# Second attention of a two-block network: two heads per step on the halves of TensorE's array, sums and factors of the head norms in fewer products

## The chip, the cores and the metric

One Trainium2 chip, one of its cores. The metric is device time in microseconds (us) of one execution, the median of three runs. TensorE (PE) does matrix products out of SBUF into PSUM banks (512 fp32 per partition each), VectorE (DVE), ScalarE (ACT) and GpSimd (POOL) work element by element, SyncE (SP) issues the transfers. Each engine executes its own instruction list strictly in the order that the scheduler wrote when the kernel was built, and waits on semaphores for the others.

## The reference, cut to what matters

Two blocks of a network over 256 tokens of 1024 features. The first (two layers of differential attention, a gated recurrence, a Fourier mixer and a feed-forward part) isn't touched. The second is a gated convolution and then this attention, `D` = 1024, 16 head slots of 64 features, three groups of dilation 1, 4 and 16:

```python
proj = h @ w_in
qkv = proj[..., :QKV_COLS].reshape(B, S, N_GROUPS, 3, HEADS_PER_GROUP, HEAD_DIM)
for g, (window, dilation) in enumerate(DILATED_GROUPS):
    q = rms_norm_2(qkv[:, :, g, 0], q_gain[g])     # norm over the 64 features of a head
    k = rms_norm_2(qkv[:, :, g, 1], k_gain[g])
    o, l = dilated_group_attention(q, k, qkv[:, :, g, 2], bias_g, window, dilation)
alpha = jax.nn.softmax(jnp.stack(lses, axis=0), axis=0)
o = jnp.sum(alpha[..., None] * jnp.stack(outs, axis=0), axis=0)
y = o.reshape(B, S, ATTN_WIDTH) * jax.nn.silu(z)
return y @ w_out
```

The merge by `alpha` equals one softmax over the keys of all three groups, and so the kernel computes it.

## The kernel before, in words

The whole kernel is one stream of large products (`gemm`, L160, and `gemm_nat`, L171): every fp32 weight is split into a high part `wH` (ACT, L138) and a low part `wL` (DVE, L140), every activation too, and a product is the sum of three fp32r products, each one record of 256 columns in this part of the kernel. The weights come by SP's queue as 512 KB halves `raw`.

`attn2` is the last part. After the gates `szz` it goes through four steps `hq` of four heads each (two pairs `i`, the heads `v` = 0, 1 of a pair in partitions 0 to 63 and 64 to 127). For each of the three groups `g` of a step:

- Queries and keys `qk` by `gemm` into a `pg` bank, ACT squares them (`sqq`), and the sums of the squares over each head's 64 features are products with the 0/1 matrix `hsel` (L1081): four products of 32 output columns, one for each pair of heads of queries and keys, two behind the queries and two behind the keys, into partitions 0, 32, 64 and 96 of a bank of `ph`.
- The values `vv` by `gemm_nat`.
- From the sums DVE makes `ms` (L1091), POOL and ACT the reciprocal root `mr` with one Newton step (L1092 to L1101), ACT and DVE split it into two parts `r` (L175, L176), and eight products with `bsel` (L1108; two parts for each of four) spread each factor over the 64 partitions of its head, into both banks of `ph`. DVE multiplies: `qhat` (L1110), `khat` (L1113).

Then the attention of the step, eight units (pair `i`, half `qt` of the query tokens, head `v`). `scores` (L1117 on) makes four fp32 products of 128 columns (`qt` = 0, "early" units below) or one of 256 and two of 128 (`qt` = 1, "late") from the 64 partitions of head `v` into a `ps` bank (there are two), DVE adds the bias tile `bt` and takes the maximum (L1133), ACT takes the exponential (L1137), DVE scales by the reciprocal of the sum (L1138, L1139): `lt`. `values` (L1142 on) transposes `lt` on PE (L1149), ACT copies it to `aT` (L1151), and four fp32 products (L1153) give 64 output partitions, `64 v` on, of the bank `pa`. Each unit's `values` is emitted one unit later than its `scores`. An fp32 product is two records ("passes") in the trace, an fp32r product or a transpose one.

The output projection `merge` (L1033 on; L160 with `yo`) of steps 0 to 2 adds into `x` (L1038, one add for six products), that of step 3 comes last (L1051, L1054).

The order on each engine is the scheduler's, from the emission order and its own estimate of when things are ready: it puts large products of the next step between the small ones of the attention. Step 3's attention has no next step; only the merges of steps 0 to 2 (24 tiles of six products) stand there to fill.

Of the kernel before, what the change touches and what calls it, by code (L numbers as in the profile page):

```python
# [9 lines left out]
F32 = mybir.dt.float32  # L10
# [36 lines left out]
for _n, _w in (("hsel", 32), ("bsel", 512)):  # L47
# [11 lines left out]
class Builder:  # L59
# [27 lines left out]
    def phase(self, *groups):  # L87
        """tags of ring() and how many tiles each has; memory goes to one group after the other"""
# [34 lines left out]
    # ---------------------------------------------------------------- weights  # L123
# [18 lines left out]
    def wload(self, src, nk=8, w=256, hold=((None, None),) * 2):  # L142
        """weights of nk * 128 rows and w columns; hold: instructions of ACT and DVE that go before each half"""
# [7 lines left out]
    def gemm(self, W, c0, acts, T, t0=0, pt=None, tag=None):  # L151
        """transposed output [128 columns, T tokens from t0]"""
# [11 lines left out]
    def gemm_nat(self, W, acts, t0, pt, p0):  # L164
        """natural output [128 tokens from t0, 256 columns]"""
# [12 lines left out]
    # ---------------------------------------------------------------- norms  # L178
# [10 lines left out]
    def sums(self, pn, c0, acc):  # L189
        """sums over the features, one per token, into columns c0.. of pn; acc = [128, 2 tiles, 128 tokens]"""  # L190
# [3 lines left out]
    def inv(self, name, src):  # L194
        """1 / sqrt(src / 1024 + eps), [128, 2]"""
# [7 lines left out]
    def spread(self, r):  # L203
        """one value per token, [128, 2], to [128, 256] on all partitions, in PSUM"""
# [13 lines left out]
    # ---------------------------------------------------------------- setup  # L218
# [26 lines left out]
    def late_setup(self):  # L245
# [12 lines left out]
        # lambda of both layers  # L258
# [13 lines left out]
        # lower bound of the forget gate in layer 1: softmax over the two layers  # L272
# [35 lines left out]
    def ada_bank(self, li, b):  # L308
        """columns 1024b.. of the modulation of layer li, for c and c_ctx"""
# [13 lines left out]
    def ada_out(self, li, pa, tiles, n):  # L323
        """n feature tiles from tiles[g] on in partitions 32g and 32g + 1"""
# [12 lines left out]
    def ada_scale(self, li, which, A, k0, k1):  # L337
        """norm weight times (1 + scale), [128, 2 sequences, 8], for feature tiles k0..k1"""
# [8 lines left out]
    def norm(self, pb, v, k, tag):  # L347
        """feature tiles k and k + 1 of the 256 tokens of sequence v, normalised"""
# [6 lines left out]
    def modulate(self, n, v, k, A, Bm, h):  # L355
        """scale and shift of what norm() gives, into high and low parts"""
# [12 lines left out]
    # ---------------------------------------------------------------- recurrent mixer  # L369
    def hgrn_seq(self, j, s, fg, kk, q, vs, S0):  # L370
        """one sequence of 256 tokens of head pair j. fg, kk: forget gates and keys, forward and backward;
        q: queries, None where only the state is wanted. Scores of tokens that part at level h of the binary
        tree over the tokens are products of a query that carries the decay from the middle of its block of 2h
        and a key that carries the decay up to there. Returns the scores' products with the values.
        K: keys with the decay to the end (plane 0) or the start (plane 1) of their block of h; Q: queries with
        the decay from the end (plane 0) or the start (plane 1); tot: products of the gates over blocks of h
        (forward, backward, forward)."""
        nc = self.nc

        def view(t, h, off, plane, bc=False):  # L380
            """[P, 2 planes, blocks of 2h, h]: half a block of each plane"""
# [4 lines left out]
        def sel(t, h, t0=0, nt=256):  # L386
            """nt tokens from t0, first halves of the blocks from plane 0 and second halves from plane 1"""
# [3 lines left out]
        def level(h, t, tots, eng):  # L391
            """blocks of 2h from blocks of h"""
# [67 lines left out]
        if s == 1:  # L460
            # state at the end of the context
# [30 lines left out]
    def hgrn(self, li, j, fg, kk, q, sg, vn, T):  # L492
# [8 lines left out]
        # head norm and gate  # L501
# [10 lines left out]
    # ---------------------------------------------------------------- first block layer  # L512
    def layer(self, li, states):
# [74 lines left out]
        def rec(j, tag=None):  # L588
            w = first[0][0] if li == j == 0 else W(8 + 2 * j)  # both forget gates of head pair j
# [12 lines left out]
            w = first[1][0] if li == j == 0 else W(6 + j)  # query and gate of head pair j  # L602
# [760 lines left out]
```

## Time and profile before

| | |
|---|---|
| median of 3 runs (lowest to highest) | 1795.1 us (1791.59 to 1797.15) |
| span of the profiled execution, first to last instruction | 1791.7 us; no time of its own is listed beside it, the lowest of the three runs is the same to 0.1 us |
| PE busy | 1731.3 us, 97% of the span |
| DVE, ACT, POOL busy | 57%, 47%, 18% |
| mean granted TensorE clock | 0.984 of 2.4 GHz |
| the chain that ended last | PE 88%, DMA 3%, DVE 3% |
| `attn2`: first product on step 0 to the last add | about 1440 to 1788 us |

A record's duration is its latency, with pipeline; what a product costs a stream of products is the distance between starts.

### The profile page before, as it was taken

What the parts mean: (1) busy time and instruction counts of PE and PEld (TensorE: products, weight loads), DVE (VectorE), ACT (ScalarE), POOL (GpSimd) and SP (SyncE); (2) the same over time, 40 slices, a digit from 0 to 9 for tenths busy, and PEclk for the clock granted to TensorE, in tenths of its full rate; (3) what the DMA queues carried; (4) which work ended last, traced back from release to release, by engine and by line L of the source; (5) the groups of instructions that cost most, each with busy time, mean ns of one, the idle gap of its engine ahead of it and who ended that gap; (6) DMA issues with size and microseconds to landing.
All of it is one profiled execution on the core that took longest, in us unless ns stands there. A gap on an engine that the chain in (4) does not pass through costs nothing.

```text
span 1791.7 us, 29942 instructions
## 1 busy us (share of the span) xinstructions
PE 1731.3 (97%) x11966; PEld 1478.6 (83%) x11966; DVE 1021.4 (57%) x1849; ACT 849.3 (47%) x1481; POOL 316.2 (18%) x412
## 2 busy tenths in 40 slices
PE   6999999888999999989999999999999999999998
PEld 3876666676878888878877899999999999898987
DVE  4457564444543454365775766777666745554646
ACT  4457454334432343254654655664444655554543
POOL 1322210121100011234310210122111202111120
PEclk9999999988999999989999899999999999999999
DMA  9433433675233222453246456465555554344441
GB/s 346 166 106 121 135 113 127 180 108 164 91 97 109 94 95 67 131 180 106 92 137 226 140 159 211 149 198 187 182 187 182 180 174 157 123 133 134 147 130 54
DMA packets 88804, 260.66 MB, mean 145 GB/s; under 512 B 8887, under 2 KB 20535, under 8 KB 88664
## 3 DMA queue, kind: packets, MB, share of 16 engines
q1 hardware_dynamic: 88664, 258.74, 45.6%
q8 instruction: 94, 1.54, 0.4%
q14 instruction: 46, 0.38, 0.1%
HBM read 252.42 MB, written 6.29 MB: 144 GB/s over the span
## 4 chain that ended last, share of the span: by engine, by line
PE 88%; DMA 3%; DVE 3%; ACT 2%; SPq 2%; issue 1%; POOL 0%; POOLq 0%; ACTq 0%; DVEq 0%
PE pg L160 35%; PE ps L160 15%; PE pu L160 8%; PE ph L160 8%; PE pg L171 7%; PE pa L319 3%; DMA araw<-in_w_ada_dram 2%; PE pa L1153 2%; PE ph L442 1%; PE ps L698 1%; PE pu L1149 1%; SPq L316 1%; PE ph L1081 1%; PE ph L1108 1%; PE pu L736 1%
## 5 line engine op out<-in xcount | busy, mean ns | idle before, releaser
L140 DVE TENSOR_TENSOR wL<-raw,wH 128x1024 fp32r<-128x1024 f32 (+2 forms) x388 | 447.2, 1180 | 286.8 <-ACT wH L138 277.8
L138 ACT CAST wH<-raw 128x1024 fp32r<-128x1024 f32 (+2 forms) x388 | 372.4, 994 | 415.9 <-PE pg L160 178.4
L160 PE MATMUL pg<-hx,wH 128*128 128x256 f32 x1152 | 215.7, 283 | 0.0
L160 PE MATMUL pg<-hm,wH 128*128 128x512 f32 (+1 forms) x736 | 209.4, 366 | 1.8 <-DVE hm L366 0.7
L160 PEld LDWEIGHTS pg<-hx,wH 128*128 128x128 f32 x1152 | 178.9, 188 | 2.5 <-issue 1.6
L160 PE MATMUL pg<-hx,wL 128*128 128x256 f32 x576 | 164.1, 285 | 0.0
L160 PEld LDWEIGHTS pg<-hm,wH 128*128 128x128 f32 x736 | 129.9, 192 | 41.4 <-issue 13.7
L160 PE MATMUL pg<-hm,wL 128*128 128x512 f32 (+1 forms) x368 | 132.4, 360 | 0.0
L160 PE MATMUL pg<-h,wH 128*128 128x256 f32 (+1 forms) x464 | 116.8, 340 | 10.4 <-ACT wH L138 8.7
L843 POOL TENSOR_TENSOR tt<-tt 128x512 f32<-128x512 f32 (+1 forms) x44 | 44.6, 1013 | 438.0 <-DVE tt L840 432.7
L160 PE MATMUL ps<-h,wH 128*128 128x256 f32 (+1 forms) x464 | 114.5, 335 | 0.0
L160 PEld LDWEIGHTS pg<-hx,wL 128*128 128x128 f32 x576 | 108.5, 188 | 5.7 <-issue 5.4
L160 PEld LDWEIGHTS pg<-h,wH 128*128 128x128 f32 x464 | 81.1, 193 | 21.8 <-ACT wH L138 9.2
L160 PEld LDWEIGHTS ps<-h,wH 128*128 128x128 f32 x464 | 80.3, 191 | 9.5
L160 PE MATMUL pg<-hid,wH 128*128 128x256 f32 (+1 forms) x360 | 81.1, 316 | 1.1 <-ACT wH L138 1.1
L160 PEld LDWEIGHTS pg<-hm,wL 128*128 128x128 f32 x368 | 70.5, 192 | 13.9 <-issue 5.0
L319 PE MATMUL pa<-araw,csil 128*32 128x256 f32 x640 | 64.7, 406 | 15.1 <-DMA araw<-in_w_ada_dram 14.5
L160 PE MATMUL pg<-h,wL 128*128 128x256 f32 (+1 forms) x232 | 78.5, 338 | 0.0
L160 PE MATMUL ps<-hid,wH 128*128 128x256 f32 (+1 forms) x344 | 77.7, 317 | 0.0
L160 PE MATMUL ps<-h,wL 128*128 128x256 f32 (+1 forms) x232 | 77.5, 334 | 0.0
L171 PE MATMUL pg<-wH,hx 128*128 128x256 f32 x384 | 76.1, 285 | 0.0
L160 PE MATMUL pu<-h,wH 128*128 128x256 f32 (+1 forms) x272 | 68.7, 339 | 4.8 <-ACT wH L138 4.8
(417 smaller groups left out, 3874.5 us busy)
## 6 DMA issues: line engine op xcount, KB each, us to landing
raw<-in_w_up_dram SPq DMA_DIRECT2D x88, 512.0 KB, 4.7
araw<-in_w_ada_dram SPq DMA_DIRECT2D x80, 512.0 KB, 5.2
raw<-in_attn_w_in_dram SPq DMA_DIRECT2D x80, 512.0 KB, 4.6
raw<-in_conv_w_in_dram SPq DMA_DIRECT2D x64, 512.0 KB, 4.6
raw<-in_w_in_dram SPq DMA_DIRECT2D x48, 512.0 KB, 4.8
raw<-in_w_down_dram SPq DMA_DIRECT2D x32, 384.0 KB, 3.5
raw<-in_w_down_dram SPq DMA_DIRECT2D x32, 320.0 KB, 2.9
raw<-in_conv_w_out_dram SPq DMA_DIRECT2D x16, 512.0 KB, 4.5
```

The source lines that it names most:

```text
L138: nc.scalar.copy(H[:, a:b], raw)
L140: nc.vector.tensor_tensor(L[:, a:b], raw, H[:, a:b].bitcast(F32), OP.subtract)
L160: nc.tensor.matmul(pt, a[:, k, c0:c0 + P], c[:, t0:t0 + T], start=n == 0, stop=n == tot - 1)
L171: nc.tensor.matmul(pt[:, p0:p0 + 256], c[:, t0:t0 + P], a[:, k, :], start=n == 0, stop=n == tot - 1)
L316: nc.sync.dma_start(raw, d["w_ada"][li, k * P:(k + 1) * P, b * 1024:(b + 1) * 1024] .rearrange("p (g c) -> p g c", g=4))
L319: nc.tensor.matmul(pa[32 * g:32 * g + 32, 0:256], self.csil[:, k, :], raw[:, g], start=k == 0, stop=k == KD - 1)
L442: nc.tensor.matmul(pt[:, v, c:c + P], l, m, start=True, stop=True)
L698: nc.tensor.matmul(pts[i][:, :n], qa[h][rr, qt * P:(qt + 1) * P], kT[h][rr, k0 * P:k0 * P + n], start=True, stop=True)
L736: nc.tensor.matmul(po[:, 0:P], aT[:, b * P:(b + 1) * P], va[kb // 2][:, kb % 2, hh * P:(hh + 1) * P], start=b == 0, stop=b == nk - 1)
L843: nc.gpsimd.tensor_tensor(tt[1], tt[0], tt[1], OP.mult)
L1081: nc.tensor.matmul(pc[32 * n:32 * n + 32, 0, 0:256], hsel, sq[:, a], start=True, stop=True)
L1153: nc.tensor.matmul(pavs[i][64 * v:64 * v + 64, qt * P:(qt + 1) * P], vv[g][:, kt, (i * 2 + v) * 64:(i * 2 + v) * 64 + 64], aT[:, k * P:(k ...
```

## The change

1. Two heads per step of the attention: `scores` and `values` now take a unit (`i`, `qt`) and do both heads `v`, their products emitted alternately. `scores` takes both `ps` banks. `values` puts the transposes of both heads into the two banks of `ph`, one `aT` tile holds both (two tiles of 4 KB in place of three of 2 KB), and the products into `pa` alternate between output partitions 0 to 63 and 64 to 127.
2. The four products of the sums are emitted together, behind the products of the values, into a `pu` bank (`sqq` gets a third buffer).
3. `hsel` puts every sum into two rows (columns 0, 1 and 16, 17 of 32). `rl` = `rh` times `low` plus `r`, with `low` 0 for the first copy and -1 for the second, holds the rounded factor in one row and the remainder in the other, so that one product with a `bsel` that has ones in both rows does what two did: four spread products for a group in place of eight. They go into `pu`, one bank for the queries and then one for the keys, where both lay in `ph` before.
4. The constant tile `cc` gets one column more (`low`).

The core of the diff (docstrings and comments were dropped elsewhere):

```diff
-        self.phase(dict(szz=4, qk=3, sqq=2, qhat=6, khat=6, vv=6, lt=4, aT=3, yo=8))
+        self.phase(dict(szz=4, qk=3, sqq=3, qhat=6, khat=6, vv=6, lt=4, aT=2, yo=8))
...
-                    sq = self.ring("sqq", [P, 2, 256])
-                    nc.scalar.activation(sq, raw[i], AF.Square)
-                    for a in range(2):
-                        n = 2 * i + a
-                        nc.tensor.matmul(pc[32 * n:32 * n + 32, 0, 0:256], hsel, sq[:, a], start=True, stop=True)
+                    sq.append(self.ring("sqq", [P, 2, 256]))
+                    nc.scalar.activation(sq[i], raw[i], AF.Square)
                 w = W(g * 12 + 8 + hq)
                 pt = self.pg()
                 t = self.ring("vv", [P, 2, 256])
                 for a in range(2):
                     self.gemm_nat(w, acts, a * P, pt, a * 256)
+                pc = self.psum("pu")
+                for n in range(4):
+                    nc.tensor.matmul(pc[32 * n:32 * n + 32, 0:256], hsel, sq[n // 2][:, n % 2], start=True, stop=True)
+                for a in range(2):
                     nc.scalar.activation(t[:, a], pt[:, a * 256:(a + 1) * 256], AF.Copy, scale=rs[:, a:a + 1])
...
-                pc = self.psum2().rearrange("p n (i t) -> p n i t", i=2)
-                rh = [self.loc(f"r{i}", [P, 256], F32R, bufs=2) for i in range(2)]
-                self.split(rh[0], rh[1], r)
-                for n in range(2):
+                rh = self.loc("r0", [P, 256], F32R, bufs=2)
+                nc.scalar.copy(rh, r)
+                rl = self.loc("r1", [P, 256], F32R, bufs=2)
+                nc.vector.scalar_tensor_tensor(rl, rh.bitcast(F32), low, r, op0=OP.mult, op1=OP.add)
+                for n, (name, gain, to) in enumerate((("qhat", g8[:, g:g + 1], qh), ("khat", self.vec("kg", g), kh))):
+                    pc = self.psum("pu")
                     for i in range(2):
-                        for c in range(2):
-                            nc.tensor.matmul(pc[:, n, i], bsel[:, 2 * n + i], rh[c], start=c == 0, stop=c == 1)
...
-            def scores(i, v, qt, b):
-                ps = self.psum("ps")
+            def scores(i, qt, bt):
+                ps = [self.psum("ps") for _ in range(2)]
                 qs = slice(qt * P, qt * P + P)
...
+                for g, o, ks in parts:
+                    for v in range(2):
+                        nc.tensor.matmul(ps[v][:, o:o + ks.stop - ks.start], qh[g][rr[v], i, qs], kh[g][rr[v], i, ks],
+                                         start=True, stop=True)
...
-                pt = self.psum2()[:, 0] if hq == 3 and len(done) % 2 else self.psum("pu")
-                for k in range(4):
-                    nc.tensor.transpose(pt[:, k * P:(k + 1) * P], lt[:, k * P:(k + 1) * P], self.ident)
-                aT = self.ring("aT", [P, 512])
-                nc.scalar.copy(aT, pt)
+                pt = self.psum2()
+                aT = self.ring("aT", [P, 2, 512])
+                for v in range(2):
+                    for k in range(4):
+                        nc.tensor.transpose(pt[:, v, k * P:(k + 1) * P], lts[v][:, k * P:(k + 1) * P], self.ident)
+                    nc.scalar.copy(aT[:, v], pt[:, v])
                 for k, (g, kt) in enumerate(blocks):
-                    nc.tensor.matmul(pavs[i][64 * v:64 * v + 64, qt * P:(qt + 1) * P],
-                                     vv[g][:, kt, (i * 2 + v) * 64:(i * 2 + v) * 64 + 64],
-                                     aT[:, k * P:(k + 1) * P], start=k == 0, stop=k == 3)
+                    for v in range(2):
+                        nc.tensor.matmul(pavs[i][64 * v:64 * v + 64, qt * P:(qt + 1) * P],
+                                         vv[g][:, kt, (i * 2 + v) * 64:(i * 2 + v) * 64 + 64],
+                                         aT[:, v, k * P:(k + 1) * P], start=k == 0, stop=k == 3)
```

The order of the instructions changes on PE and on DVE within `attn2`, and nowhere ahead of it. The first place is the attention of step 2 on PE, first pair, with the large products between them left out. Before (the number behind `ps` tells the banks' tiles, one for each head):

```order
L1123 MATMUL ps_16571<-khat_16083,qhat_16081 128x256
L1129 MATMUL ps_16571<-khat_16305,qhat_16303 128x128
L1129 MATMUL ps_16571<-khat_16527,qhat_16525 128x128
L1123 MATMUL ps_16594<-khat_16083,qhat_16081 128x256
L1129 MATMUL ps_16594<-khat_16305,qhat_16303 128x128
L1129 MATMUL ps_16594<-khat_16527,qhat_16525 128x128
```

Now, at the same late unit, and then at the late unit of the second pair:

```order
L1129 MATMUL ps_16516<-khat_16046,qhat_16041 128x256
L1129 MATMUL ps_16516<-khat_16265,qhat_16260 128x128
L1129 MATMUL ps_16516<-khat_16484,qhat_16479 128x128
...
L1129 MATMUL ps_16517<-khat_16046,qhat_16041 128x256
L1129 MATMUL ps_16517<-khat_16265,qhat_16260 128x128
L1129 MATMUL ps_16517<-khat_16484,qhat_16479 128x128
...
L1129 MATMUL ps_16616<-khat_16046,qhat_16041 128x256
L1129 MATMUL ps_16616<-khat_16265,qhat_16260 128x128
L1129 MATMUL ps_16616<-khat_16484,qhat_16479 128x128
L1112 MATMUL pu_16895<-r1_16893,bsel_13835 128x256 x2
...
L1129 MATMUL ps_16617<-khat_16046,qhat_16041 128x256
```

The code emits the products of the two heads alternately, but the list holds all of one head and then all of the other, with one large product between them at the first unit shown, two spread products and 20 large ones at the second. Over the four steps the stretches of score products between other work number 28 before and 35 now.

The second place is a unit's values on PE, the same step, now:

```order
L1155 MATMUL ph_16541<-ca_71,lt_16508 128x128 x4
L1159 MATMUL pa_16540<-aT_16542,vv_15966 64x128
...
L1159 MATMUL pa_16540<-aT_16542,vv_15966 64x128
L1159 MATMUL pa_16540<-aT_16542,vv_16185 64x128 x2
L1159 MATMUL pa_16540<-aT_16542,vv_16404 64x128 x2
L1159 MATMUL pa_16540<-aT_16542,vv_15966 64x128 x2
```

The first of the eight products is issued alone, behind the transposes, and the other seven, which alternate, some 30 rows later. So it is in 15 of the 16 units; in the last all eight stand together. Before, each of the 32 units had its four products in one stretch.

The third place is the end of PE's list, behind the last merge tile of step 2. Now:

```order
L1052 MATMUL pg<-yo,wH 128x256 x2
L1052 MATMUL pg<-yo,wL 128x256
L1159 MATMUL pa<-aT,vv 64x128 x7
L1155 MATMUL ph<-ca,lt 128x128 x8
L1159 MATMUL pa<-aT,vv 64x128 x8
L1052 MATMUL ps<-yo,wH 128x256
```

Before, the last values were spread among the products of the merges:

```order
L1153 MATMUL pa<-aT,vv 64x128 x4
L1051 MATMUL ps<-yo,wL 128x256
L1051 MATMUL ps<-yo,wH 128x256
L160 MATMUL pg<-yo,wH 128x256 x2
L160 MATMUL pg<-yo,wL 128x256
L160 MATMUL pg<-yo,wH 128x256 x2
L160 MATMUL pg<-yo,wL 128x256
L1051 MATMUL ps<-yo,wH 128x256
```

Now all products with the first half of `yo` stand ahead of the last seven products of one unit, and between the last transposes, the last values and the last 24 products nothing else is left.

## Rows read from the trace of the kernel before

**Rows 1.** The page: its head, and PE's busy time with share and records.

```profile
span 1791.7 us, 29942 instructions
PE 1731.3 (97%) x11966; PEld 1478.6 (83%) x11966; DVE 1021.4 (57%) x1849; ACT 849.3 (47%) x1481; POOL 316.2 (18%) x412
```

**Rows 2.** Windows up to step 3's last sums, and behind them: length, busy time (records).

```profile
1453.30:1737.70 284.40, 284.40 (x2267) 257.99 (x2265) 146.24 (x244) 148.75 (x248) 49.91 (x66) 1.00 0.43 139
1737.70:1791.70 54.00, 46.70 (x363) 41.30 (x359) 34.59 (x86) 19.01 (x36) 5.80 (x6) 0.99 0.22 72
```

**Rows 3.** Timeline of PE around two of the sums' products: start, us, records.

```profile
1453.33 0.28 PE L171 MATMUL pg<-wH,hx 128*128 128x256 f32 x1
1453.54 0.62 PE L1081 MATMUL ph<-sqq,cc 128*32 128x256 f32 x4
1454.10 0.38 PE L171 MATMUL pg<-wL,hx 128*128 128x256 f32 x1
1454.32 0.40 PE L171 MATMUL pg<-wH,hx 128*128 128x256 f32 x2
1454.55 0.28 PE L171 MATMUL pg<-wL,hx 128*128 128x256 f32 x1
```

**Rows 4.** Timeline of PE around the values of one head in step 3.

```profile
1777.81 0.39 PE L1051 MATMUL ps<-yo,wH 128*128 128x256 f32 x2
1778.13 1.09 PE L1153 MATMUL pa<-aT,vv 128*64 128x128 f32 x8
1779.15 0.50 PE L160 MATMUL pg<-yo,wH 128*128 128x256 f32 x2
1779.49 0.28 PE L160 MATMUL pg<-yo,wL 128*128 128x256 f32 x1
```

**Rows 5.** Timeline of PE in the recurrence: products alternating between output halves, first and last.

```profile
124.11 0.44 PE L487 MATMUL ph<-Sd,vh 128*64 128x128 f32 x4
...
124.81 0.39 PE L487 MATMUL ph<-So,vh 128*64 128x128 f32 x4
```

**Rows 6.** Timeline of PE in the modulation: four neighbouring tiles of 32 columns.

```profile
163.26 1.06 PE L319 MATMUL pa<-araw,csil 128*32 128x256 f32 x12
```

**Rows 7.** Timeline of PE: late scores of two heads, one behind the other.

```profile
1752.03 0.28 PE L160 MATMUL pg<-yo,wL 128*128 128x256 f32 x1
1752.24 0.70 PE L1123 MATMUL ps<-khat,qhat 64*128 64x256 f32 x2
...
1753.85 0.51 PE L160 MATMUL pg<-yo,wH 128*128 128x256 f32 x2
1754.19 0.28 PE L160 MATMUL pg<-yo,wL 128*128 128x256 f32 x1
```

**Rows 8.** Timeline of PE: late scores of one head alone.

```profile
1529.02 0.36 PE L171 MATMUL pg<-wH,hx 128*128 128x256 f32 x1
1529.31 0.70 PE L1123 MATMUL ps<-khat,qhat 64*128 64x256 f32 x2
...
1530.38 0.38 PE L171 MATMUL pg<-wL,hx 128*128 128x256 f32 x1
1530.61 0.28 PE L171 MATMUL pg<-wH,hx 128*128 128x256 f32 x1
```

**Rows 9.** Waits of PE from 1737.7 us on: in total, times, longest.

```profile
PE ph L1108 <- ACT r L175: 1.4, 1, 1.4
PE pg L160 <- DVE x L1038: 0.8, 2, 0.5
```

**Rows 10.** Timeline of DVE: factors of step 3's last group, from sums to split.

```profile
1738.11 0.42 DVE L1091 SCALAR_TENSOR_TENSOR ms<-ph,Rb 128x256 f32<-128x256 f32 x1 [1.26 <-PE ph L1081]
...
1746.05 0.42 DVE L176 TENSOR_TENSOR r<-mr,r 128x256 fp32r<-128x256 f32 x1 [0.39 <-ACT r L175]
```

**Rows 11.** Groups of DVE from 1737.7 us on: busy us, mean ns, idle time before.

```profile
L140 DVE TENSOR_TENSOR wL<-raw,wH 128x1024 fp32r<-128x1024 f32 x6 | 7.5, 1270 | 0.2 <-ACT wH L138 0.2
L1133 DVE CUSTOM_DVE_ANT_0 lt<-ps,bt 128x512 f32<-128x512 f32 x8 | 5.3, 684 | 0.7 <-PE ps L1129 0.7
...
L1158 DVE TENSOR_TENSOR y<-pa,szz 128x256 f32<-128x256 f32 x2 | 0.8, 424 | 2.3 <-PE pa L1153 2.3
```

More of the change, by code (lines that the diff above doesn't have):

```diff
@@ L46 @@
 _ncc = 0
-for _n, _w in (("hsel", 32), ("bsel", 512)):
+for _n, _w in (("hsel", 32), ("bsel", 512), ("low", 1)):
     _CC[_n] = (_ncc, _ncc + _w)
@@ new lines, in attn2 @@
+                nc.scalar.copy(rh, r)
[3 more added lines that the diff above has]
+                    pc = self.psum("pu")
+                    for i in range(2):
+                        nc.tensor.matmul(pc[:, i * 256:(i + 1) * 256], bsel[:, 2 * n + i], rl, start=True, stop=True)
+                    o = self.ring(name, [P, 2, 256])
+                    nc.vector.scalar_tensor_tensor(o.rearrange("p i t -> p (i t)"), raw[n].rearrange("p i t -> p (i t)"),
+                                                   gain, pc, op0=OP.mult, op1=OP.mult)
+                    to.append(o)
@@ L1119, in scores @@
+            def scores(i, qt, bt):
+                ps = [self.psum("ps") for _ in range(2)]
                 qs = slice(qt * P, qt * P + P)
-                rr = slice(64 * v, 64 * v + 64)
-                lq = [qh[g][rr, i, qs] for g in range(3)]
+                rr = [slice(64 * v, 64 * v + 64) for v in range(2)]
                 if qt:
-                    nc.tensor.matmul(ps[:, 0:256], lq[0], kh[0][rr, i, :], start=True, stop=True)
+                    parts = [(0, 0, slice(0, 256))] + [(g, (g + 1) * P, qs) for g in (1, 2)]
@@ L1124, in scores @@
                 else:
-                    nc.tensor.matmul(ps[:, 0:128], lq[0], kh[0][rr, i, 0:P], start=True, stop=True)
-                    nc.tensor.matmul(ps[:, 384:512], lq[0], kh[0][rr, i, P:256], start=True, stop=True)
-                for g in (1, 2):
-                    o = (g + 1 if qt else g) * P
-                    nc.tensor.matmul(ps[:, o:o + P], lq[g], kh[g][rr, i, qs], start=True, stop=True)
-                lt = self.ring("lt", [P, 512])
-                mx = self.sml("mx", [P, 2], bufs=4)
@@ L1132, in scores @@
-                bb = (b[:, 0:4] if qt else b[:, 1:5]).rearrange("p a c -> p (a c)")
-                nc.vector.tensor_tensor_reduce(out=lt, in0=ps, in1=bb, scale=1.0, scalar=-3.0e38, op0=OP.add,
-                                               op1=OP.max, accum_out=mx[:, 0:1])
-                nc.vector.tensor_scalar(mx[:, 1:2], mx[:, 0:1], -1.0, None, op0=OP.mult)
-                Z = self.sml("Z", [P, 2], bufs=4)
-                nc.scalar.activation(lt, lt, AF.Exp, bias=mx[:, 1:2], accum_out=Z[:, 0:1])
@@ L1138, in scores @@
-                nc.vector.reciprocal(Z[:, 1:2], Z[:, 0:1])
-                nc.vector.tensor_scalar(lt, lt, Z[:, 1:2], None, op0=OP.mult)
-                return lt
-            def values(i, v, qt, lt):
-                if v == 0 and qt == 0:
+                    parts = [(0, 0, slice(0, P)), (0, 384, slice(P, 256))] + [(g, g * P, qs) for g in (1, 2)]
+                for g, o, ks in parts:
+                    for v in range(2):
+                        nc.tensor.matmul(ps[v][:, o:o + ks.stop - ks.start], qh[g][rr[v], i, qs], kh[g][rr[v], i, ks],
+                                         start=True, stop=True)
@@ new lines, in scores @@
+                lts = []
+                for v in range(2):
+                    lt = self.ring("lt", [P, 512])
+                    mx = self.sml("mx", [P, 2], bufs=4)
+                    bb = (bt[v][:, 0:4] if qt else bt[v][:, 1:5]).rearrange("p a c -> p (a c)")
+                    nc.vector.tensor_tensor_reduce(out=lt, in0=ps[v], in1=bb, scale=1.0, scalar=-3.0e38, op0=OP.add,
+                                                   op1=OP.max, accum_out=mx[:, 0:1])
+                    nc.vector.tensor_scalar(mx[:, 1:2], mx[:, 0:1], -1.0, None, op0=OP.mult)
+                    Z = self.sml("Z", [P, 2], bufs=4)
+                    nc.scalar.activation(lt, lt, AF.Exp, bias=mx[:, 1:2], accum_out=Z[:, 0:1])
+                    nc.vector.reciprocal(Z[:, 1:2], Z[:, 0:1])
+                    nc.vector.tensor_scalar(lt, lt, Z[:, 1:2], None, op0=OP.mult)
+                    lts.append(lt)
@@ L1163, in attn2 @@
             sz = szs[hq]
-            pavs, prev, bt, done = {}, None, {}, []
-            for u in [(i, v, qt) for i in range(2) for qt in range(2) for v in range(2)] + [None]:
-                lt = None
+            pavs, prev, bt = {}, None, {}
+            for u in [(i, qt) for i in range(2) for qt in range(2)] + [None]:
+                lts = None
                 if u:
-                    i, v, qt = u
+                    i, qt = u
                     if qt == 0:
-                        bt[v] = bias_tile(hq * 4 + i * 2 + v)
-                    lt = scores(i, v, qt, bt[v])
+                        bt = [bias_tile(hq * 4 + i * 2 + v) for v in range(2)]
+                    lts = scores(i, qt, bt)
                 if prev:
                     values(*prev)
-                prev = (*u, lt) if u else None
+                prev = (*u, lts) if u else None
         for hq in range(4):
@@ L1263, in _constants @@
     cc = np.zeros((P, _ncc), f)
-    cc[0:64, 0] = 1
-    cc[64:128, 1] = 1
-    for n in range(4):
-        for v in range(2):
-            cc[32 * n + v, 32 + n * P + 64 * v:32 + n * P + 64 * v + 64] = 1
+    for v in range(2):
+        for half in range(2):
+            cc[64 * v:64 * v + 64, 16 * half + v] = 1
+            for n in range(4):
+                cc[32 * n + 16 * half + v, 32 + n * P + 64 * v:32 + n * P + 64 * v + 64] = 1
+    cc[:, 544] = np.where(i % 32 < 16, 0, -1)
     bk = _buckets()
```

20 lines of the change are left out of this document (8 added, 12 removed).

## Prediction

> **What bounds the kernel now.** I read the page first, then windows, the timeline of PE and the waits. The page shows PE busy for 97% of the span [rows 1]; a busy share alone doesn't say that PE's work sets the end. The windows do: from the first sums of `attn2` to the last ones of step 3 PE is busy for 284.40 of 284.40 us, while DVE and ACT work half of the time [rows 2]. There a product saved is time saved, as long as what PE needs next is there. Behind these sums the step without a next step remains: 54.00 us, PE busy for 46.70 [rows 2], some of it waits: 1.4 us for the factors and 0.8 us for adds [rows 9]. So I count PE's work for all of `attn2`, and then ask what waits appear in the last step.
>
> The price of an operation on PE is not its duration but the distance between starts, and a stretch of products on a part of the array pays for entering and leaving. Large products follow each other at 0.117 us: two from 1454.32 to 1454.55 [rows 3].
>
> **Sums.** From 1453.33 to 1454.32 stand two large products and one group of two sums' products: 0.99 less 0.23 is 0.75 us for a group [rows 3]. There are 24 groups (12 times two), 18.0 us. Now four products stand together, in 12 groups, one of them cut in two: 13 stretches. Do four neighbours cost more than two? The modulation puts four tiles of 32 columns side by side, and twelve passes took 1.06 us there, one alone being 0.4 [rows 6]; two at a time they would be six rounds of some 0.22, 1.5 us with the pipeline. So four go together, and a stretch costs 0.75 as before. Bounds: 0.75 and twice its inner part, 1.2. I take 0.75, the row being of the same shape: 24 x 0.75 - 13 x 0.75 = **8.2 us saved** (with 1.2: 2.4).
>
> **Spread.** 96 products become 48, full array, at the stream's pace: 48 x 0.117 = **5.6 us saved**. The keys' two must now wait until DVE has emptied the one bank (`qhat`). In steps 0 to 2, 20 to 28 large products stand between in PE's list, 2.3 us or more, and cover that; in the last step it is counted below.
>
> **Values.** From 1777.81 to 1779.49 stand four large products and one head's eight passes: 1.68 - 0.47 = 1.21 us [rows 4]. In the recurrence the products already alternate between output halves: from the first row of four passes to the last are twelve passes in 0.70 us, six slots of 0.117 for two passes each [rows 5]. So two heads take the slots of one, if they alternate. Eight slots are 0.9 us, so entering and leaving cost 0.3. Now PE's list has, for 15 of 16 units, one product alone (two slots and a switch, 0.2 + 0.3 = 0.5) and then seven, whose busier half has eight passes (1.2); the last unit has all in one stretch. Before 32 x 1.21 = 38.7, now 15 x 1.75 + 1.21 = 27.5: **11.2 us saved**. Bounds: were it no overlap, 15 x 2.7 + 2.2 = 42, 4 lost; without the cut, 19.4 saved. The row [rows 5] is the same form, so the upper part of this is unlikely.
>
> The Trainium skill, TensorEngine Tiling (Array Packing), section Theoretical Speedup, gives up to twice the speed for a dimension of 64 or less; under Key Properties it also says that a change of the tiling mode drains the engine. By the first alone the values would save 19.4 us and the total would be some 8 us lower; the trace agrees with the second (the 0.3 us for each stretch, rows 4), and that is why the cut costs most of the difference.
>
> **Scores.** The diff alternates the heads, the list doesn't: it has all of one head, large products, and then the other, except at the first unit of a step. What it costs: two heads in succession took 1752.03 to 1754.19, less three large products, 1.81 us [rows 7], since the second head starts while the first still runs; one head alone 1529.02 to 1530.61, less two, 1.36 [rows 8]. Eight slots being 0.9, a switch is 0.45 here. Before, 28 stretches: 8 with one product for each head (estimate 0.3 + 0.45 = 0.75), 6 with one head (1.36), 8 with two heads in succession (1.81), 6 others (about 1.0): 6.0 + 8.2 + 14.5 + 6.0 = 34.7. Now 35: 7 at 0.75, 16 with one head (1.36), 1 in succession, 5 alternating with three products each (0.65 + 0.45), 6 others at about 0.85: 5.3 + 21.8 + 1.8 + 5.5 + 5.1 = 39.5. That is 4.8 lost. Tiled stretches border on each other in 14 places now against 4, and share a switch of about 0.2: 2.0 back. **2.8 us lost.** Were they alternating in one stretch each, 16 x 1.36 = 21.8, 13 saved: that is a bound, which the list excludes.
>
> Transposes keep their number and their groups of four; the split on DVE, the copies, the exponentials keep shapes and counts. One column more in `cc` is loaded before the convolution, far from use. On SP's queue the last two bias tiles of a step now follow each other, with a weight half less between; the fourth waits for a reduction, and weights behind it with it. PE's work without any wait up to 1737.7 [rows 2] says that weights come with room; were it used up, this belongs to the second rival.
>
> PE's work: -8.2 - 5.6 - 11.2 + 2.8 = **-22.2 us**.
>
> **The last step.** Its factors take from the sums' products until 1746.47 (1746.05 + 0.42; `ms` began at 1738.11), 8.4 us [rows 10]. Until the first spread product PE's list has eight merge tiles and one stretch of scores now, 48 x 0.117 + 0.9 = 6.5, so some 1.5 to 2 us of wait, in place of 1.4 before [rows 9]. From the first spread product to the next unit's scores, which need the second bank, DVE's list has two splits of weights (1.27), two reductions (0.68), `qhat` and `khat` (taken as 0.68, the same 512 columns) and four adds (taken as 0.42, the 256 columns of L1158) [rows 11], 6.9 us in all, where PE's has six merge tiles (4.2), the spread (0.5) and a stretch of scores (0.75): 1.4 us of waits. At the very end PE's list has transposes, copy, last values, and then nothing: 0.9 us for the copy and 1.4 for `y` (0.42 [rows 11]), its cast and its subtraction, which before lay beside merges. Some 5.3 in place of 2.2: **3 us lost**.
>
> **Sum.** 1791.7 - 22.2 + 3 = 1772.5 for the span. The median of the runs lies 3.4 us above the profiled span (1795.1 against 1791.7): 1776. Within 0.3% (5.4 us) a measurement of this kernel can't tell a change from none.
>
> **The rivals.**
> - *As above*, 1768 to 1783: chance 0.67.
> - *Waits in steps 0 to 2.* PE works strictly in order, and each unit's scores now want both `ps` banks, each unit's transposes both banks of `ph`. If PE waits 0.7 us for each of these 12 units (a reduction's length, rows 11), 8 us are given back: 1784. Against it, nothing waited there before [rows 2], and the list leaves large products between most. Chance 0.15 (1783 to 1789).
> - *Less switching than I count*: values that take half, the cut costing nothing, save 8 us more: 1768; with no extra waits in the last step also 1765. Chance 0.08 (1760 to 1768). The 0.3 us of a stretch [rows 4] speak against it. The factor of two of the Trainium skill's TensorEngine Tiling (Array Packing), Theoretical Speedup, would come out as this case.
> - *Slower, by DVE's queue.* In front of the reduction that frees the second bank stand another reduction and a weight's split: 0.68 + 1.27 = 1.95 us. If PE waits for that at each of the 16 units, 31 us go, 12 more than the gain: 1807. It decides from 1.2 us per unit on (19 over 16). In the list that queue stands so in the last step only, four units. Chance 0.04.
> - *No overlap: the change doesn't do what it says.* Values lose 4, sums save 2.4 at most, spread saves 5.6, scores lose 3, the last step 3: 1797. Rows 5 and 6 show overlap in this kernel. Chance 0.01; the rest, 0.05, for small mixtures that end within 0.3%.
>
> **Chances and range.** Slower by over 0.3%: 0.04; within: 0.05; faster: 0.91. The range takes the first case, most of the second and the upper part of the third: 1766 to 1787.
>
> **What would show it.** Right: sums in some 13 stretches of 0.75 us; 48 spread products; a unit's seven products in 1.0 us from first to last start, starts in pairs; scores of a head in 1.3 us, no pairs, except at a step's first unit; PE full up to the last sums, and these about 18 us earlier than 1737.7; more wait behind them. Wrong: waits of PE on DVE's `mx` or `lt` in steps 0 to 2; eight slots that take 1.8 us; sums of four that take 1.2.

## The result, and the profile after

The changed kernel takes 1777.57 us (median of 4 runs, 1775.45 to 1778.72), the kernel before, run beside it, 1793.59 us (4 runs, 1791.59 to 1797.15). The ratio is 0.9908, with a 95% interval of 0.9896 to 0.9921: 16 us less. The profiled execution took 1775.45 us, with a span of 1773.6. The page of the changed kernel, its head and PE's row, which answer to [rows 1]:

```profile
span 1773.6 us, 29835 instructions
PE 1707.7 (96%) x11918; PEld 1462.1 (82%) x11918; DVE 1018.5 (57%) x1849; ACT 846.3 (48%) x1481; POOL 320.8 (18%) x412
```

The windows of the changed kernel up to the last sums of step 3, and behind them, with the columns of [rows 2]:

```profile
1460.80:1721.50 260.70, 260.70 (x2181) 239.74 (x2180) 142.30 (x242) 142.78 (x244) 54.25 (x66) 1.00 0.46 149
1721.50:1773.60 52.10, 43.38 (x356) 37.77 (x348) 34.71 (x86) 19.15 (x37) 5.06 (x6) 0.98 0.20 65
```

PE is still full up to the last sums, at a granted clock of 1.00, its upper level, and these come 16.2 us earlier (1721.5 against 1737.7). Behind them the span is 1.9 us shorter, though PE is idle for longer (8.7 us against 7.3 [rows 2]). All waits of PE in the attention lie there:

```profile
PE pg L160 <- DVE x L1039: 1.3, 3, 0.7
PE ps L1052 <- ACT yo L175: 1.0, 1, 1.0
PE ph L1155 <- ACT aT L1156: 0.7, 1, 0.7
PE pg L160 <- ACT vv L1089: 0.5, 1, 0.5
PE pa L1159 <- ACT aT L1156: 0.3, 1, 0.3
```

They add up to 3.8 us. In the kernel before they are 2.5: the two rows of [rows 9], 2.2, and a third that [rows 9] doesn't show:

```profile
PE pg L160 <- ACT vv L1087: 0.3, 1, 0.3
```

Before the last sums there is none in either kernel. Behind them, PE's list from the sums to the first spread product, and DVE's from the sums to the factors' second part:

```profile
1721.20 0.64 PE L1087 MATMUL pu<-sqq,cc 128*32 128x256 f32 x8
1721.77 0.94 PE L1129 MATMUL ps<-khat,qhat 64*128 64x128 f32 x12
...
1729.84 0.40 PE L1112 MATMUL pu<-r,bsel 128*128 128x256 f32 x2
```

```profile
1721.91 0.42 DVE L1093 SCALAR_TENSOR_TENSOR ms<-pu,Rb 128x256 f32<-128x256 f32 x1 [2.91 <-PE pu L1087]
...
1729.10 0.48 DVE L1108 SCALAR_TENSOR_TENSOR r<-r,cc,mr 128x256 fp32r<-128x256 f32 x1
```

Now the prices, from the timeline of PE (start, us, operation, records). Four sums side by side, in place of the two of [rows 3]:

```profile
1460.63 0.28 PE L171 MATMUL pg<-wH,hx 128*128 128x256 f32 x1
1460.84 0.64 PE L1087 MATMUL pu<-sqq,cc 128*32 128x256 f32 x8
1461.40 0.51 PE L160 MATMUL pg<-hx,wH 128*128 128x256 f32 x2
```

From the large product in front to the one behind are 0.77 us, exactly what two sums took (1453.33 to 1454.10 in [rows 3]); less the large product's own 0.12 that is 0.65. The spread is 48 products, as the diff says, and a pair of them takes as long as a pair of large ones (1473.84 to 1474.08 in the timeline, 0.24 us). Its line of the source view:

```profile
L1112 PE MATMUL pu<-r,bsel x48: 276/282/388, 1473.8 to 1731.6; 128*128 128x256 f32 x48
```

The values of one unit, the first product alone and then seven together:

```profile
1554.81 0.60 PE L1155 MATMUL ph<-ca,lt 128*128 128x128 f32 x4
1555.34 0.43 PE L1159 MATMUL pa<-aT,vv 128*64 128x128 f32 x2
1555.70 0.38 PE L160 MATMUL pg<-hx,wL 128*128 128x256 f32 x1
...
1558.43 0.40 PE L160 MATMUL pg<-hx,wH 128*128 128x256 f32 x2
1558.76 1.09 PE L1159 MATMUL pa<-aT,vv 128*64 128x128 f32 x14
1559.78 0.66 PE L1155 MATMUL ph<-ca,lt 128*128 128x128 f32 x4
```

Fourteen passes take 1.09 us, as long as the eight of one head in [rows 4]; inside, they start in pairs, 0.01 us apart. The scores of one head, alone between large products:

```profile
1522.66 0.40 PE L160 MATMUL pg<-hx,wH 128*128 128x256 f32 x2
1522.99 1.14 PE L1129 MATMUL ps<-khat,qhat 64*128 64x256 f32 x6
1524.06 0.39 PE L160 MATMUL pg<-hx,wL 128*128 128x256 f32 x1
```

No pairs there: six passes of one head, in 1.16 us (1524.06 less 1522.78, the start of the second large product, less 0.12).

To see all terms at once I give each product the distance from its start to that of the next product, less the time that PE stood idle in between (where it is over 0.05 us), which has a column of its own. What a large product in front of another kind takes above 0.118 us goes to that kind. From the first of the last 2,040 large products (of the weights and the merge) to the last one, in us; four small products of the norm at the start, 0.4 us, are with the large ones:

| kernel | large | sums | spread | scores | transposes | values | waits | all |
|---|---|---|---|---|---|---|---|---|
| before | 251.1 | 15.2 | 12.0 | 29.5 | 14.0 | 35.3 | 2.6 | 359.8 |
| changed | 248.7 | 8.3 | 6.6 | 32.6 | 16.5 | 23.2 | 3.8 | 339.7 |
| norms_only | 249.8 | 8.0 | 6.7 | 33.8 | 15.3 | 34.4 | 3.0 | 351.0 |
| heads_only | 248.8 | 11.5 | 12.7 | 30.7 | 16.9 | 23.5 | 4.1 | 348.3 |
| scores_alt | 250.0 | 7.7 | 6.3 | 21.6 | 13.5 | 23.9 | 2.3 | 325.4 |
| values_whole | 248.6 | 7.8 | 6.6 | 33.1 | 14.5 | 17.5 | 4.0 | 332.1 |
| values_apart | 248.7 | 7.8 | 6.6 | 33.1 | 14.5 | 25.3 | 4.0 | 340.0 |
| both_alt | 248.7 | 7.7 | 6.3 | 21.3 | 13.5 | 17.2 | 2.5 | 317.3 |

The attention is 20.1 us shorter, the span only 18.1: some 2 us were given back ahead of it. From the last `ps` product of L210 to the last `pu` product of L210 (the norms ahead of the convolution and of the attention) the same instructions in the same order took 438.4 us before (990.0 to 1428.4), and take 441.1 now; the rows of before, and then of now:

```profile
L210 PE MATMUL pu<-dg,ca x12: 271/275/275, 373.9 to 1428.4; 128*128 128x128 f32 x12
L210 PE MATMUL ps<-dg,ca x4: 421/422/582, 989.2 to 990.0; 128*128 128x128 f32 x4
```

```profile
L210 PE MATMUL pu<-dg,ca x12: 270/275/275, 370.4 to 1430.2; 128*128 128x128 f32 x12
L210 PE MATMUL ps<-dg,ca x4: 275/275/377, 988.6 to 989.1; 128*128 128x128 f32 x4
```

### The profile page after: what moved, and what is told of

Same layout as the page of the kernel before. It is cut to its first block, busy times and chain, and to the rows that moved or that the text cites. A ratio compares the mean times of both kernels' runs of the same rounds, so it can differ in the third digit from the quotient of the medians.

```text
span 1773.6 us, 29835 instructions
## 1 busy us (share of the span) xinstructions
PE 1707.7 (96%) x11918; PEld 1462.1 (82%) x11918; DVE 1018.5 (57%) x1849; ACT 846.3 (48%) x1481; POOL 320.8 (18%) x412
## 4 chain that ended last, share of the span: by engine, by line
PE 88%; DVE 3%; DMA 3%; ACT 2%; SPq 2%; issue 1%; POOL 0%; ACTq 0%; DVEq 0%
PE pg L160 35%; PE ps L160 15%; PE pu L160 8%; PE ph L160 8%; PE pg L171 7%; PE pa L319 3%; DMA araw<-in_w_ada_dram 2%; PE ps L1129 2%; PE ph L442 1%; PE ps L698 1%; PE pa L1159 1%; PE ph L1155 1%; SPq L316 1%; DVE wL L140 1%; PE pu L736 1%
## 5 line engine op out<-in xcount | busy, mean ns | idle before, releaser
L319 PE MATMUL pa<-araw,csil 128*32 128x256 f32 x640 | 64.0, 401 | 13.1 <-DMA araw<-in_w_ada_dram 11.5
L187 POOL TENSOR_TENSOR acc<-acc,y 128x256 f32<-128x256 f32 x40 | 37.4, 944 | 205.0 <-ACT y L186 192.9
```

What stands on the lines that cost most here:

```text
L187: st["last"] = i, (nc.vector if last else nc.gpsimd).tensor_tensor(st["acc"], st["acc"], sq, OP.add)
L319: nc.tensor.matmul(pa[32 * g:32 * g + 32, 0:256], self.csil[:, k, :], raw[:, g], start=k == 0, stop=k == KD - 1)
```

## The experiments

My theory: PE's work sets the time up to the last step, each stretch of products on a part of the array pays for its slots and its own entering and leaving, and two heads share slots only where the list has them alternate. Its rivals: a chain (of the factors) or waits set the time; a stretch costs its slots alone; or neighbouring passes overlap in any order.

### The halves of the change, alone

`norms_only` has the new sums and spread with the old scores and values. Its only edit beside the old functions is where the transposes go, since `pu` is taken:

```diff
-                pt = self.psum2()[:, 0] if hq == 3 and len(done) % 2 else self.psum("pu")
+                pt = self.psum("pu") if hq == 3 and len(done) % 2 else self.psum2()[:, 0]
```

> Only the first half of the change: sums as four neighbours and one spread product, the scores and values one head at a time as before (their transposes in a bank of ph instead of pu, since the sums and spreads have pu now). Theory (PE's work sets the time, and its terms add): 8.2 + 5.6 = 13.8 us less than before, about 1780, ratio 0.992. Rival (what counts is the shorter chain of the factors, so all of the gain is here): as fast as the whole change, 1777.5 or less, ratio 0.990 or less. Rival (the gain is in the paired values): no faster than 1788.

Measured: 1789.46 us (8 runs) against 1793.55, ratio 0.9974 (0.9963 to 0.9985): 4 us less, not 13.8. The table says why: sums and spread save 7.2 and 5.3 us, near the forecast, but scores cost 4.3 more and transposes 1.3 more, with code of the scores that is the same word for word. The list has changed: heads whose scores ran one behind the other before now stand alone between large products, 40 stretches of scores in place of 28. Whether the sums and the spread do that, or the other banks of the transposes, this run doesn't part. The rival of the paired values has the time right (no faster than 1788), but not the reason, since sums and spread did save 12.5 us. 8.8 us remain in the attention; 2.7 of them are lost ahead of it (992.6 to 1433.7 us between the two rows of L210, 441.1), and this execution's first 990 us were 2.6 us longer too.

`heads_only` has the new scores and values, with the sums in two groups of two and the spread with two products (in the changed kernel's banks, and `bsel` with ones in one row for each, which the cut leaves out):

```diff
+                        for a in range(2):
+                            n = 2 * i + a
+                            nc.tensor.matmul(pc[32 * n:32 * n + 32, 0:256], hsel, sq[:, a], start=True, stop=True)
...
-                nc.vector.scalar_tensor_tensor(rl, rh.bitcast(F32), low, r, op0=OP.mult, op1=OP.add)
+                nc.vector.tensor_tensor(rl, r, rh.bitcast(F32), OP.subtract)
...
-                        nc.tensor.matmul(pc[:, i * 256:(i + 1) * 256], bsel[:, 2 * n + i], rl, start=True, stop=True)
+                        for c in range(2):
+                            nc.tensor.matmul(pc[:, i * 256:(i + 1) * 256], bsel[:, 2 * n + i], (rh, rl)[c],
+                                             start=c == 0, stop=c == 1)
```

> Only the second half of the change: both heads of a pair together in scores and values, the sums in two groups of two and the spread with two products (high and low part) as before. Theory (the terms add): values 11.2 less, scores 2.8 more, 3 us of waits in the last step: 5.4 us less than before, about 1788, ratio 0.997. Rival (less switching than counted): 13 us less, 1780. Rival (waits for both banks eat it): 1794 or more, with waits of PE on DVE in the steps before the last.

Measured: 1786.66 us (6 runs), ratio 0.996 (0.9945 to 0.9976), 7 us less, as the theory has it to within 1.5 us, but by other terms: values 11.8 less, scores 1.2 and transposes 2.9 more, spread 0.7 and waits 1.5 more, large products 2.3 less, and sums 3.7 less though they are as before (16 of their 24 groups now border on other stretches or on each other). One half loses 5.6 us in scores and transposes, the other 4.1, and both together 5.6: what borders on what is a property of the whole list, and the terms don't add. The rivals that put all of the gain into one half, the factors' chain or the paired values, fall with these two: neither has it all.

### Scores that alternate in the list too

I take it that the list takes the heads apart because the two `ps` banks come free one after the other. In `scores_alt` both heads' scores go to the one tile of two banks, and the transposes to the single banks:

```diff
-                ps = [self.psum("ps") for _ in range(2)]
+                ps = self.psum2()
...
-                        nc.tensor.matmul(ps[v][:, o:o + ks.stop - ks.start], qh[g][rr[v], i, qs], kh[g][rr[v], i, ks],
+                        nc.tensor.matmul(ps[:, v, o:o + ks.stop - ks.start], qh[g][rr[v], i, qs], kh[g][rr[v], i, ks],
...
-                pt = self.psum2()
+                pt = [self.psum("ps") for _ in range(2)]
```

> The changed kernel with the scores of both heads in the one tile of two banks (ph) and the transposes in the two single banks (ps): now the list does alternate the heads, since both banks come free together. Theory (a stretch of one head costs its own slots and its own switch, and only the list kept the scores from overlapping): the 16 units' scores take some 22 us of PE in place of some 35, so 10 to 13 us less than the changed kernel: 1765 to 1768, ratio to before 0.985. Rival (the scores of a unit now wait until both heads of the one before have left the banks, 0.7 to 2 us for each of 16 units): 1777 to 1800, with waits of PE at the scores.

Measured: 1762.37 us (4 runs), ratio 0.9824 (0.9809 to 0.9838), 15 us less than the changed kernel. Its timeline of PE around the scores of a unit:

```profile
1599.54 0.28 PE L160 MATMUL pg<-hx,wL 128*128 128x256 f32 x1
1599.75 1.16 PE L1129 MATMUL ph<-khat,qhat 64*128 64x128 f32 x16
1600.84 0.50 PE L160 MATMUL pg<-hx,wH 128*128 128x256 f32 x2
```

Sixteen passes of two heads in 1.30 less 0.12, 1.18 us: what six passes of one head, with as many columns as eight of these, took above. In the table scores fall by 11.0 and transposes by 3.0. The Trainium skill, TensorEngine Tiling (Array Packing), section Theoretical Speedup, gives up to twice for a dimension of 64 or less; inside a stretch that alternates, this row agrees. No wait of PE at a score is listed: the rival of the waits falls. So the scores, where the change lost, held its largest unused gain, and one tile of two banks in place of two tiles was enough to get it.

### Values in one stretch, and not alternating

`values_whole` issues the second head's product first, whose data come last, and holds the others in order behind it; `values_apart` is the same, with four products of one head and then four of the other.

```diff
-                    for v in range(2):
-                        nc.tensor.matmul(pavs[i][64 * v:64 * v + 64, qt * P:(qt + 1) * P],
+                    for v in (1, 0):
+                        mm = nc.tensor.matmul(pavs[i][64 * v:64 * v + 64, qt * P:(qt + 1) * P],
...
+                        if k or v == 0:
+                            self.tc.keep_in_program_order(mm)
```

> The changed kernel with the unit's values in one stretch: the second head's product is issued first, and the others are held in order behind it, so that none runs alone ahead of the large products. Theory (a switch for each stretch, 0.3 us and two slots of 0.1): 15 stretches of 0.5 us fall away: 7 us less than the changed kernel, about 1770, ratio to before 0.987. Rival (a stretch costs no more than its slots): 15 x 0.2 = 3 us less at most, 1774.5 or more.

Measured: 1770.42 us (4 runs), ratio 0.9867 (0.9848 to 0.9886), 7 us less than the changed kernel; values 23.2 to 17.5 in the table, and transposes, four of which stood in front of each product that ran alone, 16.5 to 14.5. Together that is 7.7, 0.51 us for each of the 15: the theory's 0.5 is right.

> The values in one stretch per unit as in the run that held them together, but four products of one head and then four of the other, not alternating. It tells whether the alternation gives the overlap of the two column halves, or the mere neighbourhood. Theory (only passes that stand close together on different halves overlap; the scores of two heads in succession took 1.81 us where one head took 1.36): a unit's values take 1.8 to 2.0 us in place of 1.2, 16 units, 10 to 13 us more than with alternation: 1780 to 1783, ratio 0.993. Rival (a stretch of sixteen passes overlaps in any order): 1770, ratio 0.987.

Measured: 1777.24 us (4 runs), ratio 0.9912 (0.9897 to 0.9926): 7 us more than alternating, between theory and rival. The timelines of PE, the unit together and alternating, and then apart:

```profile
1567.92 0.28 PE L171 MATMUL pg<-wH,hx 128*128 128x256 f32 x1
1568.13 1.09 PE L1159 MATMUL pa<-aT,vv 128*64 128x128 f32 x16
1569.15 0.39 PE L171 MATMUL pg<-wH,hx 128*128 128x256 f32 x1
```

```profile
1567.21 0.28 PE L171 MATMUL pg<-wH,hx 128*128 128x256 f32 x1
1567.42 1.58 PE L1159 MATMUL pa<-aT,vv 128*64 128x128 f32 x16
1568.93 0.38 PE L171 MATMUL pg<-wH,hx 128*128 128x256 f32 x1
```

1.11 and 1.60 us, 0.49 apart, times 16 is 7.8. Alternation gives the overlap; but in the middle of the stretch apart the starts lie 0.05 us apart for 0.4 us, since the second head's products run beside the first one's last. That border was worth more than I had taken for it.

### Both

`both_alt` is `scores_alt` with the values of `values_whole`.

> The two that gained most put together: scores of both heads in the tile of two banks, and the unit's values held in one stretch. Theory (PE's work still sets the time up to the last step, so the terms add): 15 less than the changed kernel for the scores and 7 for the values, 1755 to 1757, ratio to before 0.979. Rival (with so little PE work left, the next thing, DVE or the weights, ends the waits): little less than with the scores alone, 1760 to 1762, with new waits of PE before the last step.

Measured: 1754.98 us (4 runs), ratio 0.9786 (0.9771 to 0.98). The terms add here, and no new wait of PE came before the last step.

### The 2.7 us ahead of the attention

All runs above take 440.7 to 441.4 us between the two rows of L210, the kernel before 438.4. There is one trace each of the kernel before again, and of the changed kernel with wider constants or with an unused tile behind them:

```diff
-for _n, _w in (("hsel", 32), ("bsel", 512), ("low", 1)):
+for _n, _w in (("hsel", 32), ("bsel", 512), ("low", 16)):
```

```diff
             nc.sync.dma_start(self.cc, self.d["cc"])
+            nc.gpsimd.memset(self.loc("pad", [P, 15], bufs=1), 0.0)
```

> The kernel before, once more, for a second trace of it. If the pace of 0.118 us between 990 and 1190 us belongs to the kernel, it is there again; if it belongs to the execution, it may be 0.120.

> The changed kernel with the new column of constants widened from 1 to 16 columns, nothing else. From 990 to 1190 us, ahead of the change's place, the large products of all kernels with the change follow each other at 0.120 us, where the profile of before has 0.118, in the same order of instructions; that gives back some 2.5 us. Theory (the one column shifts the memory addresses of all tiles behind it by 4 bytes or a multiple that divides no row of memory evenly, and products read from there at a slower pace): with 16 columns the pace is 0.118 again, 1775, ratio 0.9895. Rival (the pace belongs to the run, not to the addresses): 0.120 or a mixture, 1777.5, ratio 0.991.

> The changed kernel with one unused tile of 15 columns behind the constants in the same memory, the constants themselves at 545 columns as in the change. It tells the place of the tiles behind it from the width of the constants' transfer. Theory (places): pace between 0.117 and 0.118 us from 990 to 1190 us, as with 16 columns, and the stretch from there to the attention 5 us shorter than in the changed kernel. Rival (the transfer or the width itself): 0.120 as in the changed kernel.

> The changed kernel with 8 columns in place of 1. Tiles behind the constants then lie 32 bytes further than in the kernel before. Theory (what counts is where a row starts relative to 64 bytes, and a place of 1 column is rounded up to 8): 0.120 as in the changed kernel. Rival (only places that are no multiple of 32 bytes are slow): below 0.1185.

> The changed kernel with 32 columns in place of 1, so that tiles behind lie 128 bytes further than in the kernel before. Theory (relative to 64 bytes): 0.117 to 0.1185, as before or as with 16 columns. Rival (each shift gives another pace, by which tiles meet in the same part of the memory): any, 0.120 too.

The two rows of L210 in the second trace of the kernel before, in `low_wide`, and in `pad_tile`:

```profile
L210 PE MATMUL pu<-dg,ca x12: 270/274/275, 374.2 to 1428.6; 128*128 128x128 f32 x12
L210 PE MATMUL ps<-dg,ca x4: 275/275/377, 990.3 to 990.8; 128*128 128x128 f32 x4
```

```profile
L210 PE MATMUL pu<-dg,ca x12: 270/275/275, 375.3 to 1431.3; 128*128 128x128 f32 x12
L210 PE MATMUL ps<-dg,ca x4: 421/422/582, 995.2 to 996.0; 128*128 128x128 f32 x4
```

```profile
L210 PE MATMUL pu<-dg,ca x12: 271/275/275, 373.5 to 1428.6; 128*128 128x128 f32 x12
L210 PE MATMUL ps<-dg,ca x4: 421/422/582, 992.3 to 993.1; 128*128 128x128 f32 x4
```

437.8 us again for the kernel before, so the pace belongs to the kernel; 435.3 with 16 columns, 435.5 with one column and the tile, so it is the place of what lies behind the constants, not the transfer. `low_8` took 441.0 (990.2 to 1431.2) and `low_32` 440.7 (992.0 to 1432.7). The mean distance of large products from 1080 to 1120 us is 0.1183 us before, 0.1200 changed, with 8 and with 32 columns, 0.1167 with 16, 0.1178 with the tile. The last two put the tiles behind to the same place and the stage takes the same, yet in this window their pace isn't the same: the shift alone doesn't settle it at each moment. The clock isn't the reason. In the window from 1110 us on, PE is granted 1.00 and is busy for 118.6 us in the kernel before and in the changed one, with 994 records in the first and 986 in the second:

```profile
1110.00:1230.00 120.00, 118.64 (x994) 118.02 (x993) 88.71 (x149) 72.38 (x123) 24.39 (x31) 1.00 0.57 181
```

```profile
1110.00:1230.00 120.00, 118.63 (x986) 118.02 (x985) 88.24 (x148) 71.26 (x121) 24.57 (x31) 1.00 0.55 177
```

Timed, `low_wide` has 1772.08 us (4 runs), ratio 0.988 (0.9864 to 0.9897), 5.5 us less than the changed kernel. My rule of 64 bytes falls with `low_32`, a shift by a multiple of 64 that is slow; its rival, another pace for each shift, stands. Which operand it is, and which place is good, stays open.

`both_wide` puts the 16 columns to `both_alt`:

> The fastest so far (scores of both heads in the tile of two banks, values held in one stretch) with the column of constants widened from 1 to 16 columns. Theory (the pace of the products before the attention depends on where the tiles lie, and adds to the rest): 5 less than without the width, about 1750, ratio to before 0.976. Rival (the pace was a chance of that run): 1755, ratio 0.979.

Measured: 1749.16 us (5 runs), ratio 0.9746 (0.9733 to 0.9759), 28 us less than the changed kernel and 46 less than before, the fastest here. Its page and its waits of PE in the attention:

```profile
span 1748.5 us, 29861 instructions
PE 1683.1 (96%) x11918; PEld 1446.0 (83%) x11918; DVE 1018.7 (58%) x1849; ACT 846.1 (48%) x1481; POOL 319.5 (18%) x412
```

```profile
PE pg L160 <- DVE x L1039: 1.4, 3, 0.7
PE pa L1159 <- ACT aT L1156: 0.6, 1, 0.6
PE pg L160 <- ACT vv L1089: 0.5, 1, 0.5
PE ph L1129 <- DVE mx L1136: 0.2, 1, 0.2
```

## Why the prediction was right, step by step

- **PE bounds.** Right. No wait before the last sums, and in every experiment the time followed PE's work.
- **Sums**, 8.2 us forecast: 6.9 by the table. Four neighbours cost what two did (rows above), in 13 stretches, one of them cut.
- **Spread**, 5.6: 5.4 by the table; in `norms_only` 5.3.
- **Values**, 11.2: 12.1. The cut into one and seven, the overlap of the halves, and the 0.5 us of the product that runs alone are all seen in the rows, and `values_whole` got the 7 us back.
- **Scores**, 2.8 lost: 3.1. The mechanism (the list doesn't alternate) is right, shown by `scores_alt`; that the size is right too is luck. I had booked one head at 1.36 us, which is 1.16; with that the same sum loses 2.8 without the 2.0 that I took back for shared borders.
- **Transposes**, put at nothing since they keep their number: 2.5 lost. In 15 units a product of the values now runs alone behind four of them, and `values_whole`, without it, has 2.0 of the 2.5 back. So the cut cost more than I booked under the values.
- **Large products** had no term: 2.4 less. The table counts what the first large products behind a stretch take longer (0.34 for two at 1461.40, 0.10 above the pace) as theirs, and they are interrupted at 72 places now, 98 before; I had that in the prices of the stretches.
- **The sum on PE**, 22.2: without waits 21.3, with waits 20.1. It is this near because misses cancel: 2.5 lost on transposes and 2.4 saved on large products, neither with a term of its own.
- **The last step**, 3 us lost: by the listed waits 1.3 (3.8 against 2.5). The step that failed is the wait of 1.5 to 2 us for the factors, which didn't come. PE's list behind the last sums took 8.1 us to the first spread product (1721.77 to 1729.84 in the rows above), not 6.5, with 0.8 us of waits on `vv` and `x` in it, and the factors took 7.7 (1721.91 to 1729.58), not 8.4, so that they were there in time. DVE's queue cost 1.1 where I had 1.4, but at merges that waited for its adds, not at the scores; the end cost 2.0 where I had 2.3.
- **One column more in `cc`, costed at nothing**: wrong, 2.7 us, ahead of its first use (1470.7 us), shown by `pad_tile` and `low_wide` as a matter of place in memory.
- **Span**: 20.1 less in the attention, 2.7 more ahead of it, 0.9 less in the first 990 us, 0.2 more at the end: 18.1, and 1773.6 where I had 1772.5. The last sums came 16.2 us earlier, not 18, for what was lost ahead. The step from span to median is 4.0 us (1777.57 less 1773.6) where I had 3.4; each run that is listed with its span takes some 1.9 us more than that, so the span of the kernel before, 1791.7, doesn't belong to its lowest run.
- **Rivals.** Waits in steps 0 to 2: none came, nor in `scores_alt`, where scores want both banks in the strictest way. DVE's queue: only the 1.1 us in the last step. No overlap: excluded by the fourteen passes in 1.09 us. Less switching: no, the cut cost its price. Of the chances, that of faster adds up to 0.90, not 0.91, as the case of no overlap ends at 1797.

## What to carry to other kernels

Price a product on a full PE by the distance between starts, and count how often the stream of large products is interrupted: a stretch on part of the array costs the same with one half busy as with both, if they alternate (1.11 us for eight passes and for sixteen). Alternation in code is not alternation in the list: all of it came only when both products of a pair became ready by one event (for the scores one tile of two banks, for the values the later operand first), and these two edits were worth 22.6 us, where the change itself was worth 16. After an edit that adds memory, compare stages that it doesn't touch.

## What the runs showed that I had not expected

The pace of full-array products of one shape, with PE at a granted clock of 1.00 or nearly (0.96 to 0.98 in the first 120 us of the stage), was between 0.1167 and 0.1200 us by where tiles lie in memory, 435.3 to 441.4 us over one stage of 438, more than the whole last step's terms (5.3 in the forecast). And passes on two halves of the array overlap for 0.4 us even where all of one half is issued before all of the other.
